# A two-block transformer on one core: other queues for the copies, fox's keys before its gates, a linear attention on 128 rows, and split compression weights

## The chip, the cores and the metric

The kernel runs on one core of one Trainium2 chip. The metric is the device time of one execution in microseconds, as the median of several runs; lower is better. The profile shows one execution apart from those runs.

## The reference, cut to what matters

512 tokens of width 1024 pass through two blocks. In the first, a mixer runs two attentions side by side: eight heads of 64 with forget gates ("fox") and four heads of gated linear attention (GLA, keys of 64, values of 128, chunks of 64 tokens):

```python
q_dec = qc * exp(bc);  k_dec = kc * exp(-bc)          # bc: cumulated log gates of a chunk
A = tril(einsum('bhnck,bhnsk->bhncs', q_dec, k_dec))
o_intra = einsum('bhncs,bhnsv->bhncv', A, vc)
dS = einsum('bhnck,bhnkv->bhnkv', kc * exp(b_last - bc), vc)   # per chunk, 64 keys x 128 values
state = d[..., None] * state + ds                     # chunk after chunk
o = o_intra + einsum('bhnck,bhnkv->bhncv', q_dec, s_prev)
```

Behind it stand a cross-attention to 256 memory tokens and an MLP, then a SwiGLU layer. The second block has a differential attention (DA, eight heads, queries and keys with rotary positions) and a sparse attention (NSA, sixteen heads in two groups), whose compressed keys and values come from a small two-layer network:

```python
blocks = x_raw[:, idx] + pos[:, None, :]   # 31 windows of 32 tokens, stride 16
return gelu(blocks @ w1) @ w2              # 2048 -> 256 -> 64, for each of two groups
```

Their outputs are gated, joined and projected, and a last SwiGLU layer ends it.

## The kernel before

All activations lie with features on the partitions and 512 tokens along the free axis. Most products are made from fp32 numbers cut into a high and a low half (fp32r): a weight tile of 512 KB lands in one of the buffers `wraw` by a DMA of SyncE (`lin` and `nat`, line 180), ScalarE writes the high half of 128x512 pieces into `wspl` and VectorE the low half, and TensorE adds up three products (high with high, high with low, low with high). `lin` gives features by tokens (`lin<-x0h,wspl`, 512 columns), `nat` tokens by features (`lin<-wspl,x0h`, 256 columns). Products of plain fp32 operands appear in the trace as two instructions each.

Attention scores use a stacked form: a key tile `kd` holds the high half of a 64-row key twice, `kl` the low half, and the query stack `qu` holds high over low. These copies across partitions are DMAs made by `move` (line 371), four for `kd`, four for `kl`, four for `qu`, 64 rows each, out of a ring `r` of three buffers; all are issued from GpSimd's queue. The rotary swap (`rope`, line 434) is four DMAs of 32 rows, `tb<-ta` or `tb<-qc`, from the same queue, 26 times in all; GpSimd itself multiplies the result by the sines (line 437).

`weave` runs a main stream (the heads of an attention) against a fill (projections that later heads and stages need) and takes now from the one and now from the other by a ratio; `pipe` orders the pieces within the fill. The queues of the engines are in-order, so the order in which the two streams are written out is the order in which each engine works. In the mixer the fill is `fox_in`, the list [gates, key 0, query 0, value 0, key 1, query 1, value 1], followed by `gla_proj(0)`, the first GLA projections; the gates are two small products `s<-misc,g` and a chain on ScalarE (`tc`, `td`, with three changes of its function table) and VectorE (`cs`). A second `weave` then runs GLA against further projections.

In `gla` one tile of 128 rows holds the keys (or queries) of two heads, 64 rows each. Scores, state update and the products of the state work on 64 rows: `s<-gq,gk` for each head, `s<-glav,gkn` for each of seven chunks and each of two heads, and `o<-gq,gsp` for each chunk and head. `o<-gA,glav` uses all 128 rows.

In the second block's first stage DA is the main stream, and the fill holds its own projections (`da_key`, `da_query`, `da_value`, in the order of the list `seq`) and the pieces of NSA. Among these are `cmp_in` (a projection, four shifted copies from GpSimd's queue into a `wraw` buffer, a load of the positions `cpos` into a tile with one buffer, and two additions that write `nsv`) and `compress` (the hidden layer's weights `cw1` in four loads into `wraw`, used as plain fp32: 64 products `lin<-nsv,wraw` of 64 columns, then GELU and a second layer).

## Time and profile before

| | |
|---|---|
| median of 3 runs | 2279.53 us (2278.78 to 2280.15) |
| profiled execution | 2278.2 us, of which the span is 2276.4 us |
| TensorE (PE) busy in the span | 2222.3 us |
| VectorE (DVE) | 1278.6 us |
| ScalarE (ACT) | 967.3 us |
| GpSimd (POOL) | 371.2 us |
| mean granted TensorE clock | 0.983 |

About 1.8 us of the profiled execution lie outside its span. "Busy" of TensorE counts the time from a matmul's start to its modelled end; pieces overlap, so the price of a matmul in a stream is the distance from its start to the next one's start. A granted clock of 1.00 is 2.4 GHz, of 0.50 1.2 GHz; a value between them is a mixture of both over the stretch. Mixer: from the start to about 280 us, GLA's part from about 182 us. DA: from about 1200 to 1500 us, NSA behind it to about 1780 us.

### The profile page before, as it was taken

The page shows a single profiled execution, that of the slowest core. Times are in us where ns is not written, and L with a number is a line of the kernel's source. Part 1 is how long each engine was busy: PE and PEld are TensorE (multiplying, and loading weights), DVE is VectorE, ACT ScalarE, POOL GpSimd, SP SyncE. Part 2 cuts the span into 40 slices and gives each one's busy share as a digit, 9 for nine tenths or more (in the row PEclk, how much of TensorE's full clock was granted, in tenths as well). Part 3 has the DMA queues.
Part 4 walks back from the last instruction along what each step waited for, and adds up shares of the span by engine and source line. Part 5 has one row for each costly group of instructions (what it writes and reads, how often), then busy time and mean ns, then how long its engine had stood idle before and what let it go on. Part 6 is the DMA issues. An engine that isn't in the chain of part 4 may idle for free. (4 is left out here: it accounts for less than half of the span.)

```text
span 2276.4 us, 30717 instructions
## 1 busy us (share of the span) xinstructions
PE 2222.3 (98%) x11491; PEld 1867.7 (82%) x11491; DVE 1278.6 (56%) x2403; ACT 967.3 (42%) x1941; POOL 371.2 (16%) x569
## 2 busy tenths in 40 slices
PE   9999999999999999999999899999999999999998
PEld 8887799888888888888887788788877888888887
DVE  6565566654345444434456667778784555543543
ACT  6553455444234333323343244466675334332332
POOL 1431012100000000000005345445651000000000
PEclk9999999999999999999999899999999999999999
DMA  3441243233333333233345655512212333333322
GB/s 134 112 121 52 75 122 108 63 95 96 96 99 94 101 93 96 89 104 101 101 137 142 168 165 153 147 43 66 63 45 65 112 102 93 94 91 104 102 88 79
DMA packets 75108, 228.13 MB, mean 100 GB/s; under 512 B 12560, under 2 KB 20464, under 8 KB 74960
## 3 DMA queue, kind: packets, MB, share of 16 engines
q1 hardware_dynamic: 61392, 192.48, 27.9%
q0 software_dynamic: 12992, 33.18, 5.6%
q8 instruction: 90, 1.47, 0.3%
q14 instruction: 58, 0.48, 0.1%
q10 hardware_dynamic: 576, 0.52, 0.1%
HBM read 188.91 MB, written 4.19 MB: 85 GB/s over the span
## 5 line engine op out<-in xcount | busy, mean ns | idle before, releaser
L154 ACT ACTIVATE wspl<-wraw 128x512 fp32r<-128x512 f32 (+1 forms) x677 | 422.3, 627 | 877.6 <-PE lin L145 800.3
L148 DVE TENSOR_TENSOR wspl<-wraw,wspl 128x512 fp32r<-128x512 f32 (+1 forms) x677 | 470.0, 697 | 428.0 <-ACT wspl L154 420.8
L244 POOL TENSOR_TENSOR rqr<-rqv,mhalf 128x4 f32<-128x4 f32 (+1 forms) x21 | 20.5, 977 | 1369.2 <-DVE rqv L241 1358.6
L145 PE MATMUL lin<-x0h,wspl 128*128 128x512 f32 (+2 forms) x396 | 158.1, 400 | 2.2 <-DVE h L151 0.9
L154 ACT ACTIVATE P<-s,nm 128x128 f32<-128x128 f32 (+2 forms) x224 | 117.5, 529 | 86.1 <-DVE nm L316 73.8
L145 PE MATMUL lin<-x1h,wspl 128*128 128x512 f32 (+2 forms) x396 | 153.6, 389 | 0.0
L145 PE MATMUL lin<-x7h,wspl 128*128 128x512 f32 (+2 forms) x396 | 153.5, 388 | 0.0
L145 PE MATMUL lin<-x2h,wspl 128*128 128x512 f32 (+2 forms) x396 | 153.5, 388 | 0.0
L145 PE MATMUL lin<-x3h,wspl 128*128 128x512 f32 (+2 forms) x396 | 153.2, 388 | 0.0
L145 PE MATMUL lin<-x4h,wspl 128*128 128x512 f32 (+2 forms) x396 | 153.0, 387 | 0.0
L145 PE MATMUL lin<-x6h,wspl 128*128 128x512 f32 (+2 forms) x396 | 152.9, 387 | 0.0
L145 PE MATMUL lin<-x5h,wspl 128*128 128x512 f32 (+2 forms) x396 | 152.7, 386 | 0.0
L316 DVE TENSOR_REDUCE nm<-s 128x1 f32<-128x128 f32 (+3 forms) x208 | 105.3, 510 | 38.7 <-PE s L145 37.7
L148 DVE TENSOR_TENSOR ptl<-tr,pth 128x512 fp32r<-128x512 f32 x152 | 88.2, 597 | 19.8 <-ACT pth L154 18.6
L154 ACT ACTIVATE pth<-tr 128x512 fp32r<-128x512 f32 x152 | 74.8, 530 | 39.6 <-PE tr L342 34.6
L145 PEld LDWEIGHTS lin<-x0h,wspl 128*128 128x128 f32 (+1 forms) x396 | 75.3, 190 | 17.5 <-ACT wspl L154 3.5
L342 PE MATMUL tr<-ident,P 128*128 128x128 f32 x480 | 83.1, 283 | 4.8 <-DVE P L151 3.5
L145 PEld LDWEIGHTS lin<-x2h,wspl 128*128 128x128 f32 (+1 forms) x396 | 74.7, 189 | 15.3
L145 PEld LDWEIGHTS lin<-x1h,wspl 128*128 128x128 f32 (+1 forms) x396 | 74.9, 189 | 14.8
L145 PEld LDWEIGHTS lin<-x3h,wspl 128*128 128x128 f32 (+1 forms) x396 | 74.4, 188 | 15.2
L145 PEld LDWEIGHTS lin<-x7h,wspl 128*128 128x128 f32 (+1 forms) x396 | 74.5, 188 | 15.0 <-issue 0.3
L145 PEld LDWEIGHTS lin<-x4h,wspl 128*128 128x128 f32 (+1 forms) x396 | 74.4, 188 | 14.8
(707 smaller groups left out, 5673.2 us busy)
## 6 DMA issues: line engine op xcount, KB each, us to landing
wraw<-in_t_m SPq DMA_DIRECT2D x64, 512.0 KB, 3.8
wraw<-in_t_f1a SPq DMA_DIRECT2D x22, 512.0 KB, 3.6
wraw<-in_t_f1b SPq DMA_DIRECT2D x22, 512.0 KB, 3.5
wraw<-in_t_f2a SPq DMA_DIRECT2D x22, 512.0 KB, 3.5
wraw<-in_t_f2b SPq DMA_DIRECT2D x22, 512.0 KB, 3.5
qu<-r POOLq DMA_DIRECT2D x80, 128.0 KB, 3.1
wraw<-in_t_f1c SPq DMA_DIRECT2D x16, 512.0 KB, 3.5
wraw<-in_t_f2c SPq DMA_DIRECT2D x16, 512.0 KB, 3.5
```

What stands on the lines that cost most here:

```text
L145: self.nc.tensor.matmul(out, lhsT, rhs, start=start, stop=stop, **kw)
L148: self.nc.vector.tensor_tensor(out, in0, in1, op=op)
L154: self.nc.scalar.activation(out, in_, func, **kw)
L244: self.nc.gpsimd.tensor_tensor(r, v, self.mhalf[:, :m], op=OP.pow)
L316: self.nc.vector.tensor_reduce(nm, ps, axis=AX.X, op=OP.max, negate=True)
L342: self.nc.tensor.transpose(ps[:, n:n + 128], P(qb, kb) if callable(P) else P[:, self.po(qb) + kb * 128:self.po(qb) + (kb + 1) * 128], self ...
```

## The change

`move`, `stacks`, `dup` and `rope` get a table of queues. The copies of high halves (all of `kd` and `kbh`, two of the four of each `qu`) are issued from ScalarE's queue, those of low halves stay on GpSimd's, and the rope swaps go to SyncE's, where the weight loads are. In `fox_in` key 0 stands ahead of the gates, and `gla_proj(0)` is taken up behind value 0 rather than at the list's end. In `gla` the two heads' queries are copied apart into `gqz`, with zeros in the other head's 64 rows, and the keys into `gkz`, with zeros in the other half-chunk's rows; GpSimd writes both, by four fills and four copies for each pair of heads (16 in all). Each product of scores and of the state then runs over 128 rows, and the state update of a chunk is one product of 256 columns for two heads, followed by two `stt` of 64 rows rather than one of 128. In the compression, `cw1` goes through `wsub` (the split into halves that other weights have), the windows are split as well, and each product becomes a high one of 128 columns and a low one of 64; `cpos` and the second layer's weights are loaded early, the shifted copies go to tiles of their own, and GpSimd repeats the hidden layer for the values (`cr`).

```diff
+        self.q = {"hi": self.nc.scalar, "lo": self.nc.gpsimd, "rope": self.nc.sync}
...
-    def move(self, dst, src):
-        self.nc.gpsimd.dma_start(dst.bitcast(F32), src.bitcast(F32))
+    def move(self, dst, src, q="lo"):
+        self.q[q].dma_start(dst.bitcast(F32), src.bitcast(F32))
...
-        self.move(U[0:64, 0], hi[0:64])
+        self.move(U[0:64, 0], hi[0:64], "hi")
...
-            self.nc.gpsimd.dma_start(sw[q * 32:(q + 1) * 32], src[(q ^ 1) * 32:(q ^ 1) * 32 + 32])
+            self.q["rope"].dma_start(sw[q * 32:(q + 1) * 32], src[(q ^ 1) * 32:(q ^ 1) * 32 + 32])
...
-        yield from pipe([gates(), key(0), query(0), value(0), key(1), query(1), value(1)])
+        yield from pipe([key(0), gates(), query(0), value(0), other, key(1), query(1), value(1)])
...
+            qz = p2.tile([128, 2, 512], F32, name="gqz")
+            kz = p2.tile([128, 4, 2, 128], F32, name="gkz")
+            for j in range(2):
+                r, z = (slice(64 * x, 64 * x + 64) for x in (j, 1 - j))
+                nc.gpsimd.memset(qz[z, j], 0.0)
+                nc.gpsimd.tensor_copy(qz[r, j], qd[r])
+                nc.gpsimd.memset(kz[z, :, j], 0.0)
+                nc.gpsimd.tensor_copy(kz[r, :, j], kn[r])
...
-                    self.mm(ps[:, s], kd[r, s], qd[r, s], True, True)
+                    self.mm(ps[:, s], kd[:, s], qz[:, j, s], True, True)
...
                 ds = self.ps("s")
+                self.mm(ds[:, :256], kz[:, n // 2, n % 2], V[:, n // 2], True, True)
                 for j in range(2):
-                    h = 2 * i + j
-                    self.mm(ds[64 * j:64 * j + 64, :128], kn[half, n // 2, 64 * j:64 * j + 64],
-                            V[half, n // 2, j * 128:(j + 1) * 128], True, True)
-                self.stt(sp[:, n + 1], sp[:, n], dc[:, n:n + 1], ds[:, :128], OP.mult, OP.add)
+                    r = slice(64 * j, 64 * j + 64)
+                    self.stt(sp[r, n + 1], sp[r, n], dc[r, n:n + 1], ds[r, 128 * j:128 * j + 128], OP.mult, OP.add)
...
-                            self.mm(o[:, cc], sp[r, n], qd[r, cc], False, n == 7, skip_group_check=True)
+                            self.mm(o[:, cc], sp[:, n], qz[:, j, cc], False, n == 7, skip_group_check=True)
...
+                            self.cpos = n1.tile([128, 32], F32, name="cpos")
+                            for i in range(2):
+                                nc.sync.dma_start(self.cpos[:, 16 * i:16 * i + 16], a["cpos"][i])
...
-                w = self.wraw.tile([128, 1024], F32, name="wraw")
-                w3 = w.rearrange("p (k n) -> p k n", k=4)
-                nc.sync.dma_start(w3, a["cw1"][i][:, 4 * c:4 * c + 4])
-                yield LATER
+                W = self.wsub(a["cw1"][i][:, 4 * c:4 * c + 4])
...
-                        self.mm(pss[m], w3[:, k, m * 128:(m + 1) * 128],
-                                B[:, 4 * c + k].rearrange("p g n -> p (g n)"),
-                                c + k + m == 0, c + k == 6, skip_group_check=True)
+                        self.mm(pc[:, o:o + 128], h[:, w], B[:, 4 * c + k], c + k + m == 0, False,
+                                skip_group_check=True)
+                        self.mm(pc[:, o:o + 64], l[:, w], B[:, 4 * c + k, :64], False, c + k == 6,
+                                skip_group_check=True)
```

On TensorE, where fox's first score stands in the mixer. Before, behind the last `nat` product of query 0 (`lin<-wspl`):

```order
391 L145 MATMUL lin<-wspl,x6h 128x256
392 L145 MATMUL lin<-wspl,x7h 128x256
393 L145 MATMUL lin<-wspl,x7l 128x256
394 L145 MATMUL lin<-wspl,x7h 128x256
395 L145 MATMUL s<-kd,qu 128x128
396 L145 MATMUL s<-kl,qu 128x128
```

After, the transposes of query 0's first tile (`tr<-ident,hraw`) stand among the products of `gla_proj(0)`:

```order
365 L147 MATMUL lin<-x6h,wspl 128x512
366 L424 MATMUL tr<-ident,hraw 128x128 x8
367 L147 MATMUL lin<-x7h,wspl 128x512
368 L147 MATMUL lin<-x7l,wspl 128x512
369 L147 MATMUL lin<-x7h,wspl 128x512
370 L147 MATMUL lin<-wspl,x0h 128x256
```

What follows them up to the first score are products of `nat` (`lin<-wspl`), of which these are the last:

```order
406 L147 MATMUL lin<-wspl,x6h 128x256
407 L147 MATMUL lin<-wspl,x6l 128x256
408 L147 MATMUL lin<-wspl,x6h 128x256
409 L147 MATMUL lin<-wspl,x6l 128x256
410 L147 MATMUL s<-kd,qu 128x128
411 L147 MATMUL s<-kl,qu 128x128
```

Three `lin` and forty `nat` products (rows 367 to 409) now lie between those transposes and the score that reads the stack made from them.

On SyncE's queue, the loads around DA's first heads (`in_n_vda`: weights of DA's values; `in_t_c`: of `cmp_in`; `in_cw`: of `compress`). Before:

```order
148 L180 DMA wraw<-in_n_vda 128x1024 x2
149 L180 DMA wraw<-in_t_c 128x1024
150 L1463 DMA wraw<-in_cw 128x1024
151 L180 DMA wraw<-in_t_c 128x1024
152 L1442 DMA cpos<-in_cpos 128x16
153 L1463 DMA wraw<-in_cw 128x1024
154 L180 DMA wraw<-in_t_kda 128x1024
```

After:

```order
149 L182 DMA wraw<-in_n_vda 128x1024
150 L436 DMA tb<-ta 32x512 x8
151 L182 DMA wraw<-in_n_vda 128x1024
152 L436 DMA tb<-ta 32x512 x8
153 L182 DMA wraw<-in_t_c 128x1024
154 L182 DMA wraw<-in_cw 128x1024
155 L436 DMA tb<-ta 32x512 x8
156 L182 DMA wraw<-in_t_c 128x1024
157 L182 DMA wraw<-in_cw 128x1024 x3
158 L182 DMA wraw<-in_t_kda 128x1024
```

The load of `cpos` is gone from between the weight loads, and three pairs of rope swaps stand there.

On TensorE, where DA's first score stands. Before, behind all of value 0 and a `lin` of 24 products:

```order
5828 L145 MATMUL lin<-x6h,wspl 128x512
5829 L145 MATMUL lin<-x7h,wspl 128x512
5830 L145 MATMUL lin<-x7l,wspl 128x512
5831 L145 MATMUL lin<-x7h,wspl 128x512
5832 L145 MATMUL s<-kd,qu 128x128
5833 L145 MATMUL s<-kl,qu 128x128
```

After, among the first `nat` products of value 0:

```order
5721 L147 MATMUL lin<-wspl,x2l 128x256
5722 L147 MATMUL lin<-wspl,x2h 128x256
5723 L147 MATMUL lin<-wspl,x3h 128x256
5724 L147 MATMUL s<-kd,qu 128x128
5725 L147 MATMUL s<-kl,qu 128x128
```

DA's first score comes 108 rows earlier, with most of value 0's products still to follow it.

## Rows read from the trace of the kernel before

**Rows 1.** The page's first part: busy time, share, instructions.
```profile
PE 2222.3 (98%) x11491; PEld 1867.7 (82%) x11491; DVE 1278.6 (56%) x2403; ACT 967.3 (42%) x1941; POOL 371.2 (16%) x569
```
**Rows 2.** Mixer, stretches: length, busy us of PE, PEld, DVE, ACT, POOL, clock, DMA share, GB/s.
```profile
36.00:52.00 16.00, 12.59 (x85) 12.39 (x85) 10.17 (x23) 10.73 (x23) 4.07 (x2) 0.79 0.22 62
68.00:84.00 16.00, 10.43 (x53) 8.31 (x53) 5.53 (x15) 5.61 (x17) 7.35 (x16) 0.68 0.55 129
...
92.00:182.00 90.00, 90.00 (x631) 81.58 (x630) 57.64 (x126) 47.96 (x114) 30.47 (x48) 1.00 0.37 106
...
222.00:232.00 10.00, 10.00 (x51) 8.04 (x51) 4.65 (x11) 2.70 (x5) 1.44 (x2) 0.83 0.17 52
```
**Rows 3.** DA, the same columns: its start, three parts of that, its later course.
```profile
1230.50:1327.50 97.00, 82.69 (x412) 65.15 (x410) 63.42 (x129) 31.77 (x83) 43.02 (x74) 0.86 0.57 156
...
1238.00:1252.00 14.00, 8.77 (x35) 5.15 (x35) 11.07 (x26) 7.95 (x22) 10.04 (x19) 0.78 0.53 148
1256.00:1276.00 20.00, 14.67 (x66) 12.59 (x65) 7.61 (x15) 4.28 (x12) 7.74 (x16) 0.67 0.65 173
1312.00:1324.00 12.00, 9.30 (x43) 7.74 (x42) 9.94 (x21) 3.92 (x10) 5.28 (x9) 0.73 0.64 164
...
1330.00:1420.00 90.00, 90.00 (x580) 79.62 (x580) 67.15 (x141) 41.26 (x101) 43.98 (x76) 1.00 0.58 163
```
**Rows 4.** Waits of TensorE, over the whole span: line, releaser, us, times, longest.
```profile
PE s L145 <- DMA qu<-r: 8.1, 2, 5.4
...
PE lin L145 <- ACT tb L154: 3.4, 1, 3.4
```
**Rows 5.** Waits of SyncE's queue, over the whole span.
```profile
SPq L180 <- DVE wspl L148: 1643.3, 315, 30.8
...
SPq L1442 <- DVE nsv L148: 28.3, 1, 28.3
```
**Rows 6.** GpSimd's timeline at fox's start: start, us, what [idle before <-releaser].
```profile
57.98 4.17 POOL L371 DMA_DIRECT2D kd<-r  x8 [4.01 <-ACT r L154]
...
66.59 1.55 POOL L371 DMA_DIRECT2D kl<-r  x3 [2.40 <-DMA kd<-r]
```
**Rows 7.** A stretch, columns as in rows 2, while those copies run.
```profile
66.00:68.00 2.00, 2.00 (x19) 2.00 (x19) 0.00 (x0) 0.38 (x1) 1.40 (x3) 1.00 1.04 274
```
**Rows 8.** TensorE's timeline: one GLA head's state products, from first to last, and what follows.
```profile
254.73 0.47 PE L145 MATMUL o<-gA,glav 128*128 128x128 f32 x2
...
258.50 0.50 PE L145 MATMUL lin<-y4h,wspl 128*128 128x512 f32 x1
258.84 0.40 PE L145 MATMUL lin<-y5h,wspl 128*128 128x512 f32 x1
259.07 0.40 PE L145 MATMUL lin<-y5l,wspl 128*128 128x512 f32 x1
```
**Rows 9.** The same timeline: a chunk's state update for two heads, and its successor.
```profile
242.31 0.43 PE L145 MATMUL s<-glav,gkn 64*64 64x128 f32 x4
242.68 0.43 PE L145 MATMUL o<-gq,gsp 64*128 64x64 f32 x2
```
**Rows 10.** The same timeline: fp32 products elsewhere, each with its successor.
```profile
29.86 1.98 PE L145 MATMUL s<-misc,g 32*128 32x512 f32 x4
31.77 0.38 PE L145 MATMUL lin<-wspl,x0h 128*128 128x256 f32 x1
...
1312.75 1.95 PE L145 MATMUL lin<-nsv,wraw 128*128 128x64 f32 x16
1314.51 0.48 PE L145 MATMUL s<-kd,qu 128*128 128x512 f32 x1
```
**Rows 11.** The page's groups of weight splits: busy us, mean ns | idle before.
```profile
L154 ACT ACTIVATE wspl<-wraw 128x512 fp32r<-128x512 f32 (+1 forms) x677 | 422.3, 627 | 877.6 <-PE lin L145 800.3
L148 DVE TENSOR_TENSOR wspl<-wraw,wspl 128x512 fp32r<-128x512 f32 (+1 forms) x677 | 470.0, 697 | 428.0 <-ACT wspl L154 420.8
```
**Rows 12.** A DMA issue on ScalarE's queue near the end: start, us.
```profile
2269.32 0.38 ACTq L1553 DMA_DIRECT2D outT<-x1h  x1
```

More of the change, by code (lines that the diff above doesn't have):

```diff
@@ L570, in fill @@
             def fill():
-                yield from self.fox_in(X, rb, rn, p1, p2, y, gates, first)
-                yield from self.gla_proj(0, X, rb, rn, p0)
+                yield from self.fox_in(X, rb, rn, p1, p2, y, gates, first, self.gla_proj(0, X, rb, rn, p0))
             weave(self.fox(Y, y, p2), fill(), 5)
@@ L619, in log_sigmoids, with fox_in @@
             yield m
-    def fox_in(self, X, rb, rn, p1, p2, y, gate, first):
+    def fox_in(self, X, rb, rn, p1, p2, y, gate, first, other):
         nc, a = self.nc, self.a
@@ L664, in done @@
                 self.scaled_split(ps, self.gcol("foxk"), kh, kl)
-                K[2 * g + t] = [self.dup(z, p2.tile([128, 2, 512], F32R, name=n)) for z, n in ((kh, "kd"), (kl, "kl"))]
+                K[2 * g + t] = [self.dup(z, p2.tile([128, 2, 512], F32R, name=n), q)
+                                for z, n, q in ((kh, "kd", "hi"), (kl, "kl", "lo"))]
             yield from self.head_tiles(a["n_fqk"][2 + g], X, rn, p1, lambda t: self.foxs >= 2 * (2 * g + t) - 2, done,
@@ L807, in gla @@
                 h = 2 * i + j
-                r = slice(64 * j, 64 * j + 64)
                 o = self.ps("o")
@@ L1126, in da_key @@
         z = self.split(k1, p2, "k", hring=True, lring=True)
-        self.dak[h] = [self.dup(t, p2.tile([128, 2, 512], F32R, name=n)) for t, n in zip(z, ("kd", "kl"))]
+        self.dak[h] = [self.dup(t, p2.tile([128, 2, 512], F32R, name=n), q)
+                       for t, n, q in zip(z, ("kd", "kl"), ("hi", "lo"))]
     def da_query(self, h, X, rb, p2):
@@ L1255, in nsa_key @@
             self.N["kb"] = [p1.tile([128, 2, 2, 512], F32R, name="kb" + x) for x in "hl"]
-        for U, t in zip(self.N["kb"], (kh, kl)):
-            self.dup(t, U[:, b])
+        for U, t, q in zip(self.N["kb"], (kh, kl), ("hi", "lo")):
+            self.dup(t, U[:, b], q)
     def nsa_gates(self, X, rb, p1):
@@ L1485, in compress @@
             nc.vector.reciprocal(u, u)
-            r = 4 if i else 1
-            H = p2.tile([128, 2, 2, r, 32], F32, name=f"ch{i}", bufs=1)
-            for m in range(2):
-                self.tt(H[:, m], *(z[:, 64 * m:64 * m + 64].rearrange("p (g n) -> p g n", g=2)[:, :, None]
-                                   .to_broadcast([128, 2, r, 32]) for z in (x, u)), OP.mult)
-            w2 = p2.tile([128, 2, 128], F32, name="cw2", bufs=1)
-            nc.sync.dma_start(w2, a["cw2"][i])
+            H = p2.tile([128, 2, 64], F32, name="ch", bufs=1)
+            self.tt(H.rearrange("p m n -> p (m n)"), x, u, OP.mult)
             yield LATER
@@ L1510, in compress @@
                     ps = self.ps()
+                    H4 = p2.tile([128, 2, 4, 32], F32, name="cr", bufs=1)
+                    nc.gpsimd.tensor_copy(H4, H[:, :, None, 32 * g:32 * g + 32].to_broadcast([128, 2, 4, 32]))
                     for m in range(2):
-                        self.mm(ps[:, :64], H[:, m, g].rearrange("p r n -> p (r n)"), w2[:, m, :64], m == 0, m == 1)
+                        self.mm(ps[:, :64], H4[:, m].rearrange("p r n -> p (r n)"), w2[:, m, :64], m == 0, m == 1)
                     for j in range(2):
```

58 lines of the change are left out of this document (32 added, 26 removed).

## The prediction

> **What bounds the kernel now.** The page's first part comes first: TensorE is busy for 2222.3 us of 2276.4 [rows 1], so no other engine bounds the kernel as a whole. What can be won is the rest: idle TensorE, stretches at the lower clock, and products that could be cheaper. The stretches are read next. I take the time lost in one as its idle time plus its busy time multiplied by the share by which the granted clock falls short of 1.00; that is rough, since the clock is a mean over the stretch, but it uses the row alone.
>
> In the mixer two stretches stand out [rows 2]. From 36 to 52 us it is 3.41 + 12.59 x 0.21 = 6.0 us lost; from 68 to 84 it is 5.57 + 10.43 x 0.32 = 8.9. The table of TensorE's waits names their starts: one wait of 3.4 us of `lin` for ScalarE's `tb`, and one of 5.4 us of a score for the copies `qu` [rows 4]. The first is the gates' chain, which holds ScalarE while PSUM waits to be emptied. The second is a chain of copies: GpSimd issues eight `kd`, then `kl`, and the later `kl` wait for the ring's buffers that the `kd` still read [rows 6]. Both times the clock falls to its lower level behind the idle time, so a wait costs nearly twice its length. From 92 to 182 TensorE is busy throughout [rows 2].
>
> GLA has no such hole. Its products with the state cost more than their columns: one head's chain of four `gA` and seven `gq` products takes 258.50 - 254.73 = 3.77 us, and the first `lin` behind it 0.34 where the next takes 0.23 [rows 8].
>
> DA's start is the third place [rows 3]. Of 97 us TensorE is busy for 82.69 at a clock of 0.86. Its three bad parts lose 5.23 + 8.77 x 0.22 = 7.2 (the first two heads, with nothing woven in), 5.33 + 14.67 x 0.33 = 10.2 (starved of weights: SyncE's queue stood 28.3 us at the second `cpos` load, whose one buffer was still read [rows 5]) and 2.70 + 9.30 x 0.27 = 5.2 (a score waiting for `qu`, the other of the two in rows 4), 22.6 in all. From 1330 to 1420, with the same kind of work woven well, TensorE is busy for all of 90.00 with VectorE at 67.15 [rows 3].
>
> **The change part by part.** *Fox's start.* Key 0 ahead of the gates moves the sixteen key copies to where value 0 and `gla_proj(0)` follow them on TensorE. Query 0's transposes are then followed by 40 `nat` and three `lin` products before the first score. At the 0.12 us at which such products follow each other at the full clock (the 256 columns are half of the 0.23 in rows 8) these cover 40 x 0.12 + 3 x 0.23 = 5.5 us, against the 5.4 of the wait. The chain that has to fit (split, four copies, landing) is about as long, so I leave a stall of 0 to 1 us. The gates' chain on ScalarE is as long as before, but now value 0's and key 0's work lies around it; its 3.4 us may come back in part at another PSUM buffer. What stands against this: `gla_proj(0)` no longer fills heads 5 to 7 of fox. Those have 36% of VectorE free even in the stretch where TensorE is full (57.64 of 90 [rows 2]), so I price that at 2 us at most. Of 14.9 us lost I take 11 as won, with ends of 4 (the gates' wait returns with its slow stretch, and half of the copies' wait) and 15.
>
> *GLA on 128 rows.* A `gq` product becomes a pair of fp32 instructions of 64 columns on all rows. Such pairs run elsewhere at (1314.51 - 1312.75) / 16 = 0.11 us an instruction [rows 10]; at that price for both kinds a head's chain is 22 x 0.11 = 2.4, 1.35 less than 3.77, and 5.4 less for four heads. Some 14 exits from a group on 64 rows save 0.11 each, 1.5. The state update goes from two products of 64 rows in 0.37 us [rows 9] to one of 256 columns; from the gates' 512 columns in (31.77 - 29.86) / 4 = 0.48 an instruction [rows 10] that is 0.48 for a pair, so 14 x 0.11 = 1.5 more. The dip of the clock from 222 to 232 costs 1.7 [rows 2]; it stands in a run of such small products, and I take half as won. Sum 6.3, with ends of 2 (the extra cost is of these operands and not of 64 rows) and 9. GpSimd's 16 fills and copies and VectorE's 14 further updates are hidden: in that stretch GpSimd is busy for 1.44 and VectorE for 4.65 of 10 us [rows 2]. Without that cover the first score would wait for four fills and four copies.
>
> A rule stands against this part. In rows 9 the two heads' state updates, 64 rows and 64 columns each, take 0.37 us together, less than my 0.48 for one product on the whole array. The Trainium skill, "TensorE: Matmul & The Clock Gate", Part 3, says that products with few rows should be put into different parts of the array, where they run at the same time. The state update agrees with it; the chain of rows 8, where products on 64 rows follow each other in one accumulation, does not, so I go by the rows.
>
> *Compression and `cpos`.* The 28.3 us stand of SyncE's queue ends, since `cpos` is loaded once and early. In its place 8 weight tiles take 16 splits on ScalarE, 16 x 0.627 = 10.0 us, and 16 on VectorE, 16 x 0.697 = 11.2 [rows 11]. TensorE's work stays: 128 instructions before and 128 after, and 0.11 is the nearest row for either form. VectorE comes to 63.42 + 11.2 = 74.6 us in what were 97 [rows 3]; in 85 that would be 88%, above the 75% at which TensorE never waited from 1330 on. Each `compress` also takes its four tiles in a row, so its products come at the pace of the splits, four of 0.70 us on VectorE a tile where one tile's 16 products take 1.76 us: I leave 2 us for each of the two as a stall. Of the 10.2 lost I take 6.
>
> *DA's first heads.* The first score comes 108 rows earlier, so heads 0 and 1 have most of value 0's products woven in. Of 7.2 lost I take 5. Of the 5.2 behind the second wait for `qu` I take 2, since two of four copies leave GpSimd's queue. DA together: 13, with ends of 2 (VectorE bounds) and 20.
>
> *Queues elsewhere.* ScalarE issues 96 copies, at the 0.38 us of its one kind of issue in this trace [rows 12] 36 us, spread over stages where it is busy for 42% [rows 1]; an exponential behind one waits so long. SyncE issues 104 swaps. GpSimd loses both. Where the stage is full of TensorE work this costs nothing; against nothing as a bound on one side and a few us on the other (-3 to +4) I take a loss of 1.
>
> **How the sum stands.** 11 + 6.3 + 13 - 1 = 29.3. From the profiled 2278.2 that gives 2248.9; the median of the runs is 1.3 us higher, so 2250.
>
> **The rivals.** *VectorE takes DA's gain.* It is at 79% already in the first heads (11.07 of 14 [rows 3]), and the splits are added there. Against it speaks the stretch from 1330. DA would give 2 to 4 instead of 13: 2260.
>
> *The transfers bound, not their issue.* While the copies of fox ran, the DMA engines were full (1.04 at 274 GB/s [rows 7]); two queues that put in the same bytes don't land them sooner. Then the wait for `qu` is shortened by the new order alone, and the wait in DA stays. Fox's start gives 6 and DA 10: 2258. The Trainium skill, "DMA: Bandwidth & Descriptors", Issuing engines are not separate DMA queues, says that several issuers only save the issuers' own time; the 1.04 agrees with it for that stretch.
>
> *Products on 64 rows already overlap.* By the rule weighed above, GLA would win nothing and pay 1.5 for the state: 29.3 - 6.3 - 1.5 = 21.5, or 2258.
>
> *Slower: a swap holds the weights behind it.* SyncE's queue is in order, and a swap waits for VectorE's `ta`. The weight loads behind it then come late, as they did behind `cpos`, where one stand cost 10.2 us. There are 26 swaps; if each cost TensorE more than 29.3 / 26 = 1.13 us, the change is slower. With 1.5 each it is 26 x 1.5 - 29.3 = +10, 2289. Against it: the loads wait 315 times for VectorE's splits to free a `wraw` buffer anyhow, 5.2 us a time [rows 5], and the swap's own input comes from the same `lin` that uses those weights up.
>
> *All is won.* 15 + 9 + 20 = 44 less 1: 2237.
>
> **How the numbers follow.** The forecast, 2250 with a range of its own from 2242 to 2256, has 0.46; VectorE 0.18; the transfers 0.11; 64 rows 0.06; all won 0.09; slower 0.06; and 0.04 for several of these losses together that leave no change. Two in ten stay outside a range from 2230 to 2268, above all the slower case and the ends of the sum. About 0.2%, 4.6 us, is what a measurement of this kernel can tell from no change: faster by more 0.90, within it 0.04, slower 0.06.
>
> **What would show it.** In the profile after: no wait for `qu` above 1 us at fox's first score, and the clock at 1.00 from 36 to 92; a GLA head's chain of 2.4 us; no stand of SyncE's queue at `cpos`, and DA's start 13 us shorter. The prediction is wrong if VectorE releases TensorE's waits in DA, if `lin` waits for `wraw` behind a swap, or if `s` waits for `P` in heads 5 to 7 of fox.

## The result, and the profile after

The changed kernel takes 2258.74 us (median of 4 runs, 2252.91 to 2262.64) where the kernel before took 2279.16 beside it: a ratio of 0.9916 [0.9894, 0.9938], some 20 us. Timed once more, as "again" below, it gave 0.9923 [0.9909, 0.9936]. The forecast was 2250 with a range from 2230 to 2268. The time lies in the range, 9 us above its centre. The experiments show that one of the terms, fox's start, hardly came at all, and that one line of the change, the queue of the rotary swaps, gives by itself all that the whole change gives.

The first part of the page of after, to be read against [rows 1]:

```profile
PE 2207.5 (98%) x11463; PEld 1861.7 (82%) x11463; DVE 1287.9 (57%) x2439; ACT 979.0 (43%) x1963; POOL 279.1 (12%) x385
```

GpSimd lost 92 of 371 us: some 200 copies that it no longer issues, less the fills and copies that it now makes for GLA. TensorE still bounds. The profiled execution, 2262.64 us, is the slowest of the four; that of "again" (2257.03) is shown where the two differ.

The mixer's stretches of after (length, busy us of PE, PEld, DVE, ACT, POOL, clock, DMA share, GB/s), those of [rows 2] and one between them:

```profile
36.00:52.00 16.00, 16.00 (x123) 14.59 (x122) 10.96 (x21) 10.84 (x19) 2.32 (x5) 1.00 0.60 153
52.00:68.00 16.00, 15.16 (x84) 12.74 (x83) 13.44 (x25) 10.39 (x20) 6.16 (x5) 1.00 0.54 160
68.00:84.00 16.00, 16.00 (x130) 15.32 (x129) 6.98 (x17) 7.41 (x20) 4.62 (x9) 1.00 0.37 99
...
92.00:182.00 90.00, 84.26 (x581) 73.77 (x581) 56.82 (x132) 49.01 (x120) 24.74 (x38) 0.98 0.30 83
...
222.00:232.00 10.00, 10.00 (x74) 9.34 (x73) 6.89 (x19) 2.60 (x5) 2.57 (x3) 1.00 0.17 54
```

The two holes at fox's start are gone: TensorE is full at 1.00 from 36 to 52 and from 68 to 84. But from 92 to 182, where it was busy for all of 90.00, it now idles for 5.7 us at 0.98. The holes were moved as much as filled.

The waits of TensorE in after (line, releaser, us, times, longest), to be read against [rows 4]:

```profile
PE s L147 <- ACT P L156: 7.1, 10, 1.8
PE lin L147 <- DVE tc L1463: 3.5, 1, 3.5
...
PE lin L147 <- ACT y6h L156: 2.8, 2, 2.1
...
PE lin L147 <- ACT tb L156: 1.3, 1, 1.3
PE s L147 <- DMA qu<-r: 1.2, 2, 0.6
```

The wait for `qu` fell from 8.1 us to 1.2 and that for `tb` from 3.4 to 1.3. Grown is the wait for `y6h`, behind GLA (1.4 us in before). New is one of 3.5 us that the table puts down to the compression's windows (`tc`); what stood behind it is shown under "What the high halves cost".

DA's first 170 us, in before, after and "again", in this order:

```profile
1195.00:1365.00 170.00, 155.69 (x856) 129.85 (x856) 108.63 (x220) 58.40 (x140) 77.79 (x135) 0.92 0.57 158
1195.00:1365.00 170.00, 159.07 (x899) 136.08 (x899) 123.06 (x251) 72.46 (x171) 43.35 (x61) 0.92 0.60 163
1195.00:1365.00 170.00, 156.32 (x941) 134.05 (x940) 126.31 (x258) 74.91 (x179) 43.98 (x63) 0.96 0.61 168
```

The count of TensorE's instructions is a rough measure here, since they are not of one length: 43 to 85 more were done in the same time. VectorE worked 14 to 18 us more there, with the added splits, and TensorE still got through more.

By the stages' ends, in the profiled executions of after and of "again", the mixer gained 6.8 and 8.6 us, DA 5.4 and 9.3, and NSA behind it 6.7 and 6.8. Stages whose code is alike differ by up to 2 us between executions, so smaller differences of one profile mean nothing. The profile of before is itself on the long side in the mixer: from 36 to 52 and from 68 to 84 its clock is 0.79 and 0.68, and 0.89 and 0.79 in two kernels below with the same code there (the compression alone, and the swaps alone), which end the mixer 1.6 and 1.3 us ahead of it.

Part of the gain is the clock. The mean granted clock of the runs is 0.985 in before, taken beside "again", and 0.989 in "again"; as an estimate, 0.004 x 2276 = 9 us of the 17.6 are time that TensorE no longer spends at the lower level.

One thing that was told ahead needs a correction. The kernel is built with `schedule_with_timeline_sim=True` (line 1682 of the kernel before): the build reorders instructions by times of its own. An edit to one queue, with every loop left alone, can therefore also move the order on all engines. Where that matters below, it is said.

### The profile page after: what moved, and what is told of

Its sections match the earlier page's. It is cut to its first block, busy times and chain, and to the rows that moved or that the text cites. A ratio compares the mean times of both kernels' runs of the same rounds, so it can differ in the third digit from the quotient of the medians.

```text
span 2260.9 us, 30848 instructions
## 1 busy us (share of the span) xinstructions
PE 2207.5 (98%) x11463; PEld 1861.7 (82%) x11463; DVE 1287.9 (57%) x2439; ACT 979.0 (43%) x1963; POOL 279.1 (12%) x385
## 4 chain that ended last, share of the span: by engine, by line
PE 91%; DVE 3%; DMA 2%; ACT 2%; issue 1%; ACTq 1%; SPq 0%; POOL 0%; DVEq 0%; POOLq 0%
PE lin L147 78%; PE s L147 6%; PE o L147 4%; PE tr L344 2%; PE tr L147 2%; DMA kd<-r 1%; ACTq L373 1%; DVE ptl L150 0%; ACT P L156 0%; DVE wspl L150 0%; DMA tb<-ta 0%; DVE nm L318 0%; ACT pth L156 0%; DMA kbh<-r 0%; ACT tb L156 0%
## 5 line engine op out<-in xcount | busy, mean ns | idle before, releaser
L156 ACT ACTIVATE wspl<-wraw 128x512 fp32r<-128x512 f32 (+1 forms) x693 | 431.9, 626 | 864.1 <-PE lin L147 809.8
L150 DVE TENSOR_TENSOR wspl<-wraw,wspl 128x512 fp32r<-128x512 f32 (+1 forms) x693 | 477.4, 692 | 408.5 <-ACT wspl L156 401.7
L246 POOL TENSOR_TENSOR rqr<-rqv,mhalf 128x4 f32<-128x4 f32 (+1 forms) x21 | 20.4, 971 | 1363.5 <-DVE rqv L243 1316.0
L147 PEld LDWEIGHTS lin<-x6h,wspl 128*128 128x128 f32 (+1 forms) x396 | 74.2, 187 | 14.6
```

Source lines behind the costliest of these rows:

```text
L147: self.nc.tensor.matmul(out, lhsT, rhs, start=start, stop=stop, **kw)
L150: self.nc.vector.tensor_tensor(out, in0, in1, op=op)
L156: self.nc.scalar.activation(out, in_, func, **kw)
L246: self.nc.gpsimd.tensor_tensor(r, v, self.mhalf[:, :m], op=OP.pow)
```

## The four parts, each alone in the kernel before

The change has four parts, each of which can be put alone into the kernel before. My sum gives them 6.3 us (GLA), 11 (order in `fox_in`), 6 (compression and `cpos`) and, for the queues, 2 in DA less 1 elsewhere. The 5 for DA's first heads I had put on the earlier first score, without saying which part brings it; the traces show that it is the queues (below).

**GLA on 128 rows** (`gqz`, `gkz`, the joint state update; nothing else):

```diff
-                    self.mm(ps[:, s], kd[r, s], qd[r, s], True, True)
+                    self.mm(ps[:, s], kd[:, s], qz[:, j, s], True, True)
...
-                            self.mm(o[:, cc], sp[r, n], qd[r, cc], False, n == 7, skip_group_check=True)
+                            self.mm(o[:, cc], sp[:, n], qz[:, j, cc], False, n == 7, skip_group_check=True)
```

> The kernel before, with the linear attention on 128 rows as the only change (zeros in queries and keys, one state update for two heads). The prediction's sum gives 6.3 us less than before, the last of the state's products about 6 us earlier and everything behind it shifted by the same. The rival that products on 64 rows already overlap gives 1 to 2 us more than before. A head's chain of eleven products should take 2.4 us instead of 3.77.

Measured: 2270.4 against 2276.94, ratio 0.997 [0.9961, 0.998], 6.5 us. TensorE's timeline shows one head's chain, first and last lines and what follows:

```profile
252.01 0.47 PE L145 MATMUL o<-gA,glav 128*128 128x128 f32 x2
...
254.47 0.48 PE L145 MATMUL s<-y4h,wspl 128*128 128x512 f32 x1
```

From 252.01 to 254.47 are 2.46 us, where [rows 8] had 3.77 (the forecast was 2.4). The dip from 222 to 232 is gone as well. Part of this is given back behind GLA, where less work is left to cover the last heads' norm:

```profile
259.96 0.51 PE L145 MATMUL lin<-y6h,wspl 128*128 128x512 f32 x1 [2.12 <-ACT y6h L154]
...
262.00:282.00 20.00, 17.62 (x62) 13.28 (x61) 17.18 (x38) 13.18 (x29) 0.70 (x1) 0.76 0.18 56
```

The wait for `y6h` was 0.67 us in before, and the clock from 262 to 282, where the mixer ends, 0.91. That products on 64 rows win nothing in such a chain is settled. So is, roughly, the size of the work saved: TensorE's busy time times the mean clock, a rough measure of its work, is 2222.3 x 0.983 = 2185 us in before and 2202.7 x 0.992 = 2185 with the swaps alone, but 2214.6 x 0.984 = 2179 here and 2207.5 x 0.987 = 2179 in after. Where the 6.5 us are won is not shown: in the profiles this kernel is only 2.0 us ahead at the mixer's end, hardly more than the two kernels whose mixer is that of before (1.6 and 1.3), and 5.2 at the end.

**The order in `fox_in`** alone (key 0 ahead of the gates, `gla_proj(0)` behind value 0):

```diff
-        yield from pipe([gates(), key(0), query(0), value(0), key(1), query(1), value(1)])
+        yield from pipe([key(0), gates(), query(0), value(0), other, key(1), query(1), value(1)])
```

> The kernel before, with only the order of fox's projections changed (key 0 ahead of the gates, the first linear-attention projections behind value 0). The prediction's sum gives 11 us less. The other theory, from the profile of the changed kernel, is that the work moved forward is missing later: the last heads of fox run without a fill and TensorE idles there; then the holes at 36 to 84 us are gone (15 us), but 5 to 10 us of idle appear between 120 and 185 us, and the sum is 5 to 8 us less than before.

Measured: 2275.76, ratio 0.9997 [0.9986, 1.0008]. Eleven microseconds were forecast, and about one came, which can't be told from none. From 36 to 52 and from 68 to 84 TensorE is full at 1.00, as in after; other windows are not (columns as above):

```profile
52.00:68.00 16.00, 13.73 (x69) 11.38 (x69) 10.04 (x17) 9.31 (x17) 4.99 (x5) 0.89 0.44 128
...
140.00:160.00 20.00, 18.58 (x97) 15.53 (x96) 7.47 (x14) 6.87 (x14) 7.66 (x16) 0.91 0.90 219
160.00:182.00 22.00, 19.35 (x125) 14.76 (x124) 16.04 (x42) 14.66 (x42) 7.82 (x15) 1.00 0.00 1
```

In before these three stretches were full at 1.00. The first heads got their cover from `gla_proj(0)`, the last heads lost it, and fox ended within 0.1 us of before.

**Compression and `cpos`** alone:

```diff
-                w = self.wraw.tile([128, 1024], F32, name="wraw")
-                w3 = w.rearrange("p (k n) -> p k n", k=4)
-                nc.sync.dma_start(w3, a["cw1"][i][:, 4 * c:4 * c + 4])
-                yield LATER
+                W = self.wsub(a["cw1"][i][:, 4 * c:4 * c + 4])
...
-        pos = p2.tile([128, 16], F32, name="cpos", bufs=1)
-        nc.sync.dma_start(pos, a["cpos"][i])
+        pos = self.cpos[:, 16 * i:16 * i + 16]
```

> The kernel before, with only the compression changed (split weights, positions and second-layer weights loaded early). The prediction gives 6 us less in the differential attention, since SyncE's queue no longer stands at the second load of the positions. If VectorE takes that back, 0 to 2 us less. Nothing should change before 1180 us.

Measured: 2271.89, ratio 0.9982 [0.9972, 0.9991], 4 to 5 us. The size is near the 6 forecast, but its place is not: SyncE's stand at `cpos` is gone, and yet DA itself gained 1.3 us in the profile, no more than executions differ. The stretch to which I had put the stand's loss is no better without it:

```profile
1256.00:1276.00 20.00, 15.26 (x56) 10.93 (x56) 16.07 (x35) 8.93 (x24) 9.83 (x18) 0.59 0.45 118
```

By my formula it loses 4.74 + 15.26 x 0.41 = 11.0 us, where before lost 10.2.

**The queues** alone (high halves to ScalarE, rope swaps to SyncE):

```diff
+        self.q = {"hi": self.nc.scalar, "lo": self.nc.gpsimd, "rope": self.nc.sync}
```

> The kernel before, with only the queues of the copies changed (high halves on ScalarE's queue, rotary swaps on SyncE's). The prediction has 2 us of gain in the differential attention and a loss of 1 elsewhere, so within 3 us of before. The rival that the transfers bound gives no gain in the first heads of the differential attention, and copies that land later than before (over 4 us for the high key copies against 2.6). The rival of held weights gives a time above before. A gain of 5 us or more would say that GpSimd's queue itself was the bound, most of all in the sparse attention, where the changed kernel won 6.8 us that no term of the sum foresaw.

Measured: 2270.6, ratio 0.9974 [0.9964, 0.9984]: 6.3 us won. In the profile DA gained 8.7 us and NSA 4.8, and the mixer lost 2.4, little more than executions differ by. DA's first score stands 108 of TensorE's instructions earlier in DA than in before, exactly as in after; with GLA or fox's order alone it doesn't move, with the compression alone it comes 14 later. So the 5 us for DA's first heads belong to this part, and my sum gives it 5 + 2 - 1 = 6 in all.

The medians' differences add up to 6.5 + 1.2 + 5.1 + 6.3 = 19.1, against 20.4 and 17.6 for the whole. That looks like a sum of four parts. The next runs show that it isn't one.

## Which queue it was

Two theories stood: that the swaps' move frees GpSimd's queue, or that the high halves' move does. Each was undone in after, and the first was made alone in before.

Swaps back to GpSimd, all else as in after:

```diff
-        self.q = {"hi": self.nc.scalar, "lo": self.nc.gpsimd, "rope": self.nc.sync}
+        self.q = {"hi": self.nc.scalar, "lo": self.nc.gpsimd, "rope": self.nc.gpsimd}
```

> The changed kernel with the rotary swaps back on GpSimd's queue; high halves stay on ScalarE's. The queues alone won 6.3 us over before, which the sum had at about 1. If the 104 swaps on GpSimd's queue (0.51 us each, 52 us in a queue that also issues the copies and scales P) were what it is relieved of, this loses 3 to 6 us against the changed kernel (14 to 17 less than before instead of 20). If it was the copies of the high halves, this changes by under 2 us.

Measured: 2269.82, ratio 0.9978 [0.996, 0.9997]. Only 5 to 6 us of the 20 are left, although fox's order, GLA and the compression are all in. GpSimd's timeline at DA's start (start, us, operation), one line of the chain of waits, and VectorE's timeline where that swap lands:

```profile
1205.13 2.01 POOL L436 DMA_DIRECT2D tb<-ta  x4 [2.20 <-DVE tc L150]
1207.13 2.07 POOL L373 DMA_DIRECT2D kl<-r  x4
1209.17 1.99 POOL L436 DMA_DIRECT2D tb<-ta  x4
...
1209.17 5.79 DMA tb<-ta
...
1214.34 0.69 DVE L150 TENSOR_TENSOR r<-tc,r 128x512 fp32r<-128x512 f32 x1 [4.25 <-DMA kd<-r]
1214.95 0.68 DVE L150 TENSOR_TENSOR ta<-lin,rstdb 128x512 f32<-128x512 f32 x1
```

The second group of swaps stands behind four copies of `kl` in the same in-order queue, and the chain runs through it: VectorE's next `ta` needs that swap landed, and 23 products of `lin` on TensorE wait for that `ta`. But at this place the four copies cost next to nothing: VectorE stood until 1214.34 for `kd`, which ScalarE issues, and `ta` follows `r` by 0.61 us, as VectorE's instructions do elsewhere. The profile shows that a swap can stand behind copies that are needed later, and not that the 11 to 14 us between this kernel and after were lost so.

High halves back to GpSimd, all else as in after:

```diff
-        self.q = {"hi": self.nc.scalar, "lo": self.nc.gpsimd, "rope": self.nc.sync}
+        self.q = {"hi": self.nc.gpsimd, "lo": self.nc.gpsimd, "rope": self.nc.sync}
```

> The changed kernel with the copies of the high halves back on GpSimd's queue; the swaps stay on SyncE's. If the copies' issue was the bound, this loses 3 to 6 us against the changed kernel. If the swaps were, under 2 us. If three queues at once only make the transfers of the differential attention's first heads slower (the high key copies land after 4 to 7 us there, and VectorE waits for the ring they read), this is faster than the changed kernel by 2 to 4 us, and that wait is gone from the profile.

Measured: 2255.26, ratio 0.9901 [0.9882, 0.992]. Nothing is lost; against after's two ratios it is at least as good. The other direction is the stronger one, a single line in before:

```diff
-            self.nc.gpsimd.dma_start(sw[q * 32:(q + 1) * 32], src[(q ^ 1) * 32:(q ^ 1) * 32 + 32])
+            self.nc.sync.dma_start(sw[q * 32:(q + 1) * 32], src[(q ^ 1) * 32:(q ^ 1) * 32 + 32])
```

> The kernel before, with one line changed: the 104 rotary swaps are issued from SyncE's queue. If GpSimd's in-order queue was what all the gain of the queues hangs on, this wins what all queues together won over before (6.3 us) or a little more, and swaps land after their issue of 0.33 us each without key copies ahead of them. If the high halves' move matters too, it wins under 4 us. If a swap holds weights behind it on SyncE's queue, it is slower than before.

Measured: 2251.84, 2254.76 and 2256.89 us (a fourth run took 4412 us and is left out), ratio 0.9905 [0.989, 0.9919]. One line gives all that the whole change gives. In the profile it lies in DA and NSA, 19.7 us in the one and 4.9 in the other, and nothing in the mixer, whose waits for `qu` (5.0 us) and `tb` (3.4) are still there. Half of it is the clock: 0.990 as the mean of the three runs, 0.985 in before beside them, an estimate of 0.005 x 2276 = 11 us. The window of this kernel over DA's start, as above:

```profile
1195.00:1365.00 170.00, 161.42 (x973) 137.64 (x972) 115.83 (x244) 65.22 (x161) 61.52 (x100) 0.97 0.61 170
```

973 instructions of TensorE where before had 856. SyncE's queue does what the slower rival feared. Its timeline in the one-line kernel, and three windows, the last with TensorE's wait in it:

```profile
1201.85 5.04 SPq L434 DMA_DIRECT2D tb<-ta  x8
...
1211.66 17.01 SPq L434 DMA_DIRECT2D tb<-ta  x12
...
1249.14 0.33 SPq L1442 DMA_DIRECT2D cpos<-in_cpos  x1
...
1268.20 11.45 SPq L434 DMA_DIRECT2D tb<-ta  x8
...
1230.00:1248.00 18.00, 15.44 (x84) 11.86 (x83) 15.49 (x35) 9.43 (x26) 10.99 (x20) 1.00 0.64 189
1248.00:1264.00 16.00, 15.86 (x100) 13.33 (x100) 11.51 (x26) 5.91 (x16) 3.08 (x6) 1.00 0.62 183
1280.00:1296.00 16.00, 11.87 (x45) 7.71 (x46) 8.76 (x23) 5.67 (x14) 3.94 (x7) 0.68 0.74 186
...
1285.95 0.66 PE L145 MATMUL lin<-x0h,wspl 128*48 128x512 f32 x1 [3.04 <-ACT wspl L154]
```

Twelve swaps hold the weight loads for 17 us, and TensorE is busy throughout (18.00 of 18 us from 1211 to 1229). The queue then waits another 17.3 us at `cpos`, which this kernel still loads late. During that stand TensorE idles for 2.56 of 18 us, nearly all of it in two waits for the softmax's `P`, and right behind it is busy for 15.86 of 16. So this stand at `cpos` doesn't by itself starve TensorE. The eight swaps at 1268 do hold TensorE up: the weights of NSA's gates (`in_t_gns`) leave the queue behind them, at 1280.66, and TensorE waits 3.04 us for the split of these weights. By my formula the stretch from 1280 to 1296 loses 4.13 + 11.87 x 0.32 = 7.9 us; how much of the clock's fall there is due to this wait isn't shown, since a wait of 2.19 us for `P` stands just before it.

What isn't separated: the edit also moved the built order. DA's first score stands 48 of TensorE's instructions earlier than in before; up to 1221 us the order is the same, and from there on, through DA and NSA, much of it differs. The same holds for the kernel with the swaps put back, from 1211 us on. Where the order is still the same nothing is won: the one-line kernel is 1.3 us ahead at the mixer's end and still 1.3 at 1221. Nor do the waits of before name the queue: from 1195 to 1365 VectorE waits 1.0 us for GpSimd's `tb` and for no copy at all, and in the one-line kernel 10.2 us for `tb`, more and not less. Of TensorE's waits in that stretch, 14.3 us in all, the one of 2.7 for `qu` goes, and with it one of 2.2 for `in_cw` and one of 2.8 that the table puts down to nothing ("issue"). How much of the 20 us is the queue and how much the order that comes with it stays open; a run with the order held fixed wasn't tried.

**What the high halves cost.** With the swaps on SyncE, before's code gives 0.9905 [0.989, 0.9919] with the high halves on GpSimd and 0.9974 [0.9964, 0.9984] with them on ScalarE: some 15 us lost, with intervals far apart. In after's code it is 0.9901 [0.9882, 0.992] against 0.9916 and 0.9923: 3 to 5 us, with intervals that overlap. Here too the built order moves with the queue. The traces show both sides. In fox it is better with ScalarE's queue: the stretch from 52 to 68 is at 13.73 us and 0.89 where GpSimd issues the high halves (the order alone, above; the same in after with them put back), and at 15.16 and 1.00 in after. In DA it hurts. A copy in after's chain of waits, ScalarE's issue of four of them, how long those took to land from 1200 to 1250, an instruction of VectorE that stood for one, and TensorE's wait behind it:

```profile
1239.70 7.49 DMA kd<-r
...
1203.87 2.79 ACTq L373 DMA_DIRECT2D kd<-r  x4
...
kd<-r ACTq DMA_DIRECT2D x12, 128.0 KB, 4.5
...
1247.32 0.69 DVE L150 TENSOR_TENSOR r<-tc,r 128x512 fp32r<-128x512 f32 x1 [3.93 <-DMA kd<-r]
...
1249.26 0.50 PE L147 MATMUL lin<-x0h,wspl 128*128 128x512 f32 x1 [3.50 <-DVE tc L1463]
```

Issued by GpSimd the same copies landed in 2.6 us in before, 3.5 with the swaps alone moved and 3.8 in after with the high halves put back; from ScalarE's queue it is 4.3 to 4.6 in four profiles (after, "again", the queues alone, the swaps put back). From 1195 to 1490 VectorE waited 6.3 to 10.9 us for `kd` in these four and 0 to 2.7 where GpSimd issues it (in before, with the compression alone, with the swaps alone, and in after with the high halves put back). Their ring `r` has three buffers, so the next split stands until they have landed, and in VectorE's in-order queue everything stands behind it, here the split of the weights that TensorE's product at 1249.26 needs. The `tc` which the table names is only the fill of 0.07 us that ended last. With the high halves back on GpSimd no `kd` is among the long pieces of that chain. A deeper ring, the direct test, wasn't tried for want of room in SBUF.

## Three attempts at what was left

**`gla_proj(0)` back at the end of fox's list**, the step that had cost the last heads their cover:

```diff
-        yield from pipe([key(0), gates(), query(0), value(0), other, key(1), query(1), value(1)])
+        yield from pipe([key(0), gates(), query(0), value(0), key(1), query(1), value(1), other])
```

> The changed kernel with the first linear-attention projections at the end of fox's fill again; key 0 stays ahead of the gates. The theory that the early projections are missing under heads 4 to 6 of fox: those get 86, 32 and 29 products again instead of 20, 0 and 0, the idle time from 120 to 182 us (7.7 us in the changed kernel) shrinks to under 3, but heads 0 and 1 get none, and 3 to 6 us appear there: within 3 us of the changed kernel. If the early heads' waits are short, since their copies no longer stand in one queue, it is 3 to 5 us faster than the changed kernel.

Measured: 2259.49, ratio 0.9928 [0.9902, 0.9953], the same as after. Two of its windows:

```profile
68.00:84.00 16.00, 14.37 (x78) 11.47 (x79) 9.27 (x27) 8.97 (x29) 5.87 (x12) 0.79 0.22 56
...
120.00:182.00 62.00, 60.29 (x384) 52.60 (x383) 37.97 (x80) 33.18 (x76) 11.37 (x22) 0.97 0.33 91
```

The late heads are covered better and the hole at head 1 is back. Counting the products of `lin` and `nat` that lie between the heads' scores says why: from head 3's first score to head 4's there are 294 of them in before, 275 in after and 248 here, since key 1's second tile may start only when head 3 has. The order of the list decides which heads go bare, not how many.

**GLA woven more slowly**, so that more projections are left beside its last heads:

```diff
-            weave(self.gla(Y, y2, p1, self.newpool("gla2", 2, c)), fill(), 1.5)
+            weave(self.gla(Y, y2, p1, self.newpool("gla2", 2, c)), fill(), 1.0)
```

> The changed kernel with one number changed: the ratio by which the linear attention is woven with its projections, 1.0 for 1.5, which leaves nine products of the output projection instead of six, six of them behind the last normalization, between the last head's products with the state and the first product that needs this head's pair. In the changed kernel TensorE waits there for 2.1 us and the clock falls. If the gain of the linear attention is given back at this tail, this wins 2 to 4 us over the changed kernel. If not, nothing changes (under 1 us).

Measured: 2255.98, ratio 0.9929 [0.9896, 0.9963], six runs of which two lie at 2272 and 2273 with a mean clock of 0.982 against 0.990 to 0.992. TensorE's waits behind GLA:

```profile
252.94 0.51 PE L147 MATMUL lin<-y6h,wspl 128*128 128x512 f32 x1 [0.20 <-ACT y6h L156]
...
259.50 0.50 PE L147 MATMUL lin<-y7h,wspl 128*128 128x512 f32 x1 [2.69 <-ACT y7h L156]
```

The wait for `y6h` goes from 2.12 to 0.20, and one of 2.69 for `y7h` takes its place. No gain can be told.

**The clock in DA.** After's profile has a stretch in which TensorE never idles and still loses some 9 us to the clock; another execution of the same kernel, "again", doesn't. First after, then "again":

```profile
1292.00:1300.00 8.00, 8.00 (x48) 7.29 (x48) 6.97 (x14) 5.49 (x13) 1.93 (x4) 0.65 0.95 268
1300.00:1308.00 8.00, 8.00 (x34) 7.19 (x34) 4.48 (x11) 3.48 (x9) 0.00 (x0) 0.50 0.42 133
...
1292.00:1300.00 8.00, 8.00 (x68) 7.31 (x67) 6.96 (x14) 5.63 (x12) 3.36 (x7) 1.00 0.93 249
1300.00:1308.00 8.00, 7.60 (x43) 6.53 (x43) 7.23 (x18) 4.11 (x10) 0.00 (x0) 1.00 0.66 208
```

68 and 43 instructions against 48 and 34. Ahead of the fall TensorE works through 24 products of 48 columns (NSA's gates) and 24 of the compression, so I moved the gates away from the compression:

```diff
-                                          [self.cmp_in(0, X, rb, n1)],
+                                          [self.cmp_in(0, X, rb, n1), self.nsa_gates(X, rb, n1)],
...
-                                          [self.compress(1, n1), self.nsa_gates(X, rb, n1)],
+                                          [self.compress(1, n1)],
```

> The changed kernel with the sparse attention's gates (24 products on 48 columns of weights) taken up beside the first projection of the compression and no longer between its second and third part. In two of four profiled executions of this order the clock fell at 1294 us without any idle time before it, behind those 24 products and 24 narrow ones of the compression, and 8 us were lost; in the other two it did not fall. If that neighbourhood is what tips the clock, the clock stays at 1.00 from 1285 to 1315 us and the median is 2 to 5 us below the changed kernel's, with less spread. If not, the median is within 1 us of it.

Measured: 2262.43, ratio 0.9937 [0.9925, 0.9949], not better. The clock fell all the same:

```profile
1290.00:1300.00 10.00, 8.32 (x45) 6.45 (x43) 9.12 (x27) 5.15 (x17) 0.57 (x1) 0.95 0.37 102
1300.00:1310.00 10.00, 9.03 (x42) 8.64 (x41) 7.66 (x20) 4.47 (x10) 2.79 (x5) 0.50 0.59 167
1310.00:1320.00 10.00, 10.00 (x41) 8.90 (x41) 5.30 (x11) 3.84 (x9) 0.00 (x0) 0.50 0.41 132
```

The edit wins nothing, but it doesn't settle the theory: here TensorE idled for 1.68 of the 10 us before the fall, in waits for `P`, which it didn't in after. What tips the clock there stays open.

**All three together** (high halves on GpSimd, GLA woven at 1.0, gates moved), and after itself beside it:

> The changed kernel with three of the edits found here together: all copies on GpSimd's queue and only the rotary swaps on SyncE's, the linear attention woven at 1.0, the sparse attention's gates moved. If each does what its own run suggests, 3 to 6 us less than the changed kernel (24 to 27 less than before); if they cover the same holes, the same as the changed kernel.

> The changed kernel itself once more, on the same chip as the others of this group, as what they are compared with. Its four runs so far gave 2252.9 to 2262.6. In its first profile the differential attention won 5.4 us over before, in two later kernels with the same code there 12.6 and 15.3; if that is one fall of the clock that comes and goes, its runs here spread over 8 to 10 us as well and the profile shows 12 to 15 us won there where the clock did not fall.

Measured: 2260.78, ratio 0.9926 [0.9914, 0.9938], and 2258.08, ratio 0.9923 [0.9909, 0.9936]. The combination is no better than after. The kernel before with its one changed line is as good as after in time, with intervals that overlap, and far the simpler.

## Why the prediction was right, and where its steps failed

The direction and the range were right. Alone, three of the four parts gave about what the sum has for them: 6.5 for 6.3 (GLA), 4 to 5 for 6 (compression), 6.3 for 6 (queues with DA's first heads). The fourth, fox's start, gave 1.2 for 11, and the shortfall from 29.3 to some 20 is as large as this one miss. Part of that agreement is luck, since the parts aren't independent: the swaps alone give the whole gain, and 5 us of it lie in NSA, of which the forecast didn't speak.

Of the signs named ahead, the wait for `qu`, the clock from 36 to 92, GLA's chain and the end of the stand at `cpos` came as said. DA is shorter by 5 to 9 us and not by 13. Of the signs against it, no wait for `P` came in fox's late heads (0.5 us in all from 100 to 185), but 5.7 us in many small waits; and VectorE does release two of TensorE's waits in DA, of 3.5 and 2.5 us.

- *Fox's start, 11.* This term failed, at the step "`gla_proj(0)` no longer fills heads 5 to 7 of fox ... so I price that at 2 us at most". I argued from VectorE's free share, but the later heads need products of TensorE to lie under their softmax. By my own formula the last stretches of the order-only kernel, 140 to 182, lose 1.42 + 18.58 x 0.09 + 2.65 = 5.7 us, against nothing before, and the stretch from 52 to 68, 2.27 + 13.73 x 0.11 = 3.8. The loss itself was also read high: in the execution of the compression alone the two stretches lose 3.41 + 12.59 x 0.11 = 4.8 and 5.29 + 10.71 x 0.21 = 7.5, together 12.3 and not 14.9. Alone the order gave 1.2 us. In after's two profiles fox's end came 6.6 and 7.6 us earlier, and 4.5 with the high halves back on GpSimd, so ScalarE's queue is at most a part of it; the interaction wasn't in the sum.
- *GLA, 6.3.* The mechanism held (3.77 to 2.46 us a chain), and the size agrees (6.5 alone, and some 6 us less work of TensorE). Not foreseen was the wait behind GLA that gives a part back: I had priced the products and not what lay under them.
- *The rule on products with few rows.* Its rival falls: by it GLA would have lost 1.5 us. In the state update alone it has a point, since one product for two heads starts at 238.06 and its successor at 238.49, 0.43 us against 0.37. The Trainium skill, "TensorE: Matmul & The Clock Gate", Part 3, on putting small products into different parts of the array, isn't contradicted by the chain, since there they follow each other in one accumulation.
- *Compression and `cpos`, 6.* Alone it gave 4 to 5, but the step by which I priced it failed: with the stand gone, the stretch that it was to have starved loses 11.0 us instead of 10.2.
- *DA's first heads, 5.* The first score's 108 instructions come with the queues alone and are no measure of the gain: the swaps alone move it by 48 and win 20 us, the queues of all copies move it by 108 and win 6.3.
- *Queues elsewhere, -1.* "GpSimd loses both" was noted and priced at nothing, since GpSimd is busy for 16% of the span. The swaps' move alone is worth some 20 us, 5 of them in NSA; by which way, the queue or the order built with it, stays open. Against it ScalarE's issue, at 0.70 us a copy and not my 0.38, and the later landing of `kd` cost DA a part.
- *Slower: a swap holds the weights.* The mechanism is there. Twelve swaps over 17.01 us cost TensorE nothing, eight others a wait of 3.04 us in a stretch that loses 7.9; the gain outweighs it.
- *VectorE takes DA's gain.* It took the added splits and let TensorE do more in the same time. The longer of the two waits that it releases is its stand for `kd`, not its own work; the other, for `P`, has its like in before (3.1 us in two).
- *The transfers bound, not their issue.* At fox's start the runs don't decide it: the wait for `qu` goes with the new order alone, as this rival says, but also with the queues alone, where the stretch from 68 to 84 is at 14.26 us and 1.00 instead of 10.43 and 0.68. In DA, where it was to stay, it fell from 2.7 us to 1.2. The Trainium skill, "DMA: Bandwidth & Descriptors", Issuing engines are not separate DMA queues, says that several issuers save the issuers' own time alone. No run here contradicts it, since none separates the issuers' time from the order built with it.

At DA's start some 12 us of work stand in GpSimd's queue in before without a gap, from 1234.85 to 1247.25; these are the first of it. I should have read it as a list of what stands before what (start, us, operation):

```profile
1234.85 2.01 POOL L434 DMA_DIRECT2D tb<-ta  x4 [3.04 <-DVE tc L148]
1236.86 2.06 POOL L371 DMA_DIRECT2D kd<-r  x4
1238.89 2.07 POOL L371 DMA_DIRECT2D kl<-r  x4
1240.91 1.02 POOL L434 DMA_DIRECT2D tb<-ta  x2
1241.90 1.06 POOL L371 DMA_DIRECT2D qu<-r  x2
1242.91 1.02 POOL L434 DMA_DIRECT2D tb<-ta  x2
1243.92 1.32 POOL L437 TENSOR_TENSOR tb<-tb,sint 128x512 f32<-128x512 f32 x1
```

The next swap is issued in two halves with a pair of `qu` between them, behind eight key copies. The multiplication at 1243.92 is that of the first swap, issued from 1234.85: the second's last pair, issued at 1242.91, can't have landed yet, at 2.2 us from issue to landing (the median from 1200 to 1260). By the same figure the first swap had landed at about 1238.6 (an estimate), so its multiplication stood some 5 us behind copies. That it delayed anyone is not shown: VectorE waits 1.0 us in all for these products.

## What to carry to other kernels

The busy share of an engine that issues copies says little about what moving its copies is worth: GpSimd was busy for 16%, and moving its 104 swaps won 20 us. List what stands in the queue where TensorE waits, try each kind of copy on another queue by itself, and look at what the built order does along with it. A fill that is moved forward leaves a hole where it was, so price what it covered by TensorE's work and not by the free share of another engine. And when parts made one at a time add up to the whole, that isn't yet a proof: put the smallest one in alone, and take it alone out.

## What the runs showed of the hardware

Issuing a copy took 0.70 us each on ScalarE's queue (2.79 for four), 0.63 on SyncE's (5.04 for eight) and about 0.5 on GpSimd's. The clock can fall to 0.50 in a stretch in which TensorE never idles, from 1292 to 1308 in after, while another execution of the same kernel runs it at 1.00; runs of one kernel, after, spread over 10 us (2252.91 to 2262.64) with mean clocks from 0.987 to 0.992.
